# One layer of a mixed-sequence encoder on one core: the S5 outputs and their gate placed beside the recurrent chain, the gate's result kept on chip, the two halves of the mixing exchanged

## Chip, cores and metric

One core of a Trainium2 chip. The metric is the device time of one execution in microseconds (us), median of several runs. The kernel as it stood takes 880.22 us (three runs, 878.32 to 882.06).

## What is computed

One encoder layer in float32 over 512 tokens of width 1024, with a memory of 256 tokens. Cut to what matters here:

```
h = rmsnorm(x) ; u, q, k, v, z, beta, a = split(h @ w_in)
# S5: two linear recurrences (forward, backward) over u, then
y = scan_f(u) + scan_b(u) + d * u
g = gelu(y)
y_s5 = rmsnorm(g * sigmoid(g @ w_glu + b_glu))              # 512 x 512
# gated delta net: 4 heads of 128, chunks of 64, both directions
for each chunk:  v_new = u_i - w_i @ S
                 o_i   = (q_i * exp(g_i)) @ S + qk_i @ v_new
                 S     = S * exp(g_last) + k_i' @ v_new
y_gdn = rmsnorm_per_head(o_f + flip(o_b)) * silu(z)         # 512 x 512
x = x + concat(y_s5, y_gdn) @ w_out                         # "the mixing"
x = x + cross_attention(rmsnorm(x), rmsnorm(mem))
x = x + hierarchical_moe(rmsnorm(x))                        # 32 experts, 2 per token
out = rmsnorm(x)
```

## The kernel before

The program is written as generators that each yield after a small piece of work. `weave((g1, n1), (g2, n2), ...)` (L44) draws from them in the ratio of the numbers, and this gives the program order. The order on each engine is then set by a scheduler in the kernel's build, which takes program order as priority and moves an instruction ahead where its own model finds an engine free; it also places the tiles, in pools on four stacks (`left`, `r1`, `r2`, `r3`; a pool opened where another was closed reuses its place, and its first write waits for the last readers of what lay there). Each engine then runs its list in order, and so does SP's list, which holds nearly all the DMA issues.

The part of the program around the change, in program order:

1. **The chain** (`gdn_chain`, L818 on): 8 chunk steps of the delta net, each in two half-steps of two heads. In each, PE forms k^T S and q^T S (L863), DVE the right-hand side `r` (L864), PE multiplies with the inverted chunk matrix `lhc` (L869), ACT copies to `vn` (L870), PE forms the state update (L880), DVE adds it (L883). It uses PSUM banks 3 to 7. `out(b)` (L824 to L838) forms the block's output with 16 small matmuls of `qkd` and `vn` (L831, L832) and calls `gdn_out` (L897 to L917): square (ACT, L904), reduce (DVE, L905, L906), a power on POOL (L907), a product (DVE, L908), four transposes (PE, L911), the load of the gate `zs` from scratch (one buffer `ozs`, L915), the product (DVE, L916) and the store of the result to `gd_scr[b]` (L917). Blocks 1 and 2 come out after the seventh step, 0 and 3 after the eighth.
2. Beside it in the weave: the memory's keys and values (`mem_kv`: weights of `xa_wk` and `xa_wv` through the ring `wst`, PE L163) and the S5 recurrence (`s5_rec`, 62 steps on DVE, L441 to L444). Ratio 20 to 9 to 47.
3. After the weave `r1` is closed. **`s5_out`** (L447 on): 8 groups `gg`, each with one load `cal` (L453), ACT and POOL work that lays out `hc` (L463, L464) and 12 matmuls (L473 to L475) with the tables `tz`; these come in two halves of eight loads each (L457, one buffer), and then 16 transposes (L484) give `gt`. It uses PSUM banks 0 and 1.
4. **`mix_weights`** for the delta-net half of `w_out`: 8 pieces, each a load `mst` (SP, L930), a high part (ACT, L931) and a low part (POOL, L932).
5. **`s5_glu`** (L491 on): 4 rounds `m` of 4 matmuls with `wglu` (L502), a sigmoid (ACT, L504), a product (DVE, L506), a square (ACT, L508), 4 matmuls with ones (L510), a scaled copy (ACT, L512) and a store to `s5_scr[m]` (L513).
6. **The mixing**: `mix_act` loads each block back (L944) and splits it in a high part (ACT, L945) and a low part (DVE, L946); `mix` makes 12 matmuls of 512 columns per block and half of the output (L169 to L171). First the delta-net half, 4 blocks by 2 halves; then the `r` stacks are closed, the S5 half's activations and weights are loaded and split (4 `mxs`, 8 `mst`), and the S5 half is mixed, together with the transposes for the cross-attention (`xattn_in`).

Of the kernel before, what the change touches and what calls it, by code (L numbers as in the profile page):

```python
# [9 lines left out]
F32 = mybir.dt.float32  # L10
# [54 lines left out]
class Enc:  # L65
# [85 lines left out]
    def wsplit(self, src, w, lo_eng):  # L151

        st = self.wcols(src, w)
        hi = self.wp.tile([P, 8, w], F32R, name="whi", bufs=2)
        lo = self.wp.tile([P, 8, w], F32R, name="wlo", bufs=2)
# [18 lines left out]
    def stage_a(self):  # L174
# [5 lines left out]
        with tc.tile_pool(name="xp", bufs=1) as xp:  # L180
# [8 lines left out]
            def first_weights():  # L189
                for c0 in (0, P):  # L190
                    self.pre[c0] = self.wsplit(self.w_in(c0, P), P, nc.gpsimd)
                self.w_g = self.wp.tile([P, 8, 16], F32, name="wg", bufs=1)
# [14 lines left out]
    def proj_u(self):  # L207
        nc = self.nc
        scr = self.u_scr
        for m in range(4):  # L210
            ps = self.proj(m * P)
            u = self.wp.tile([P, 8, 64], F32, name="ut", tag="ut", bufs=1)
# [278 lines left out]
    def s5_glu(self):  # L491
        nc, sp, A = self.nc, self.s5g, self.A
        gt = self.gt
        wg = sp.tile([P, 4, T], F32, name="wglu")
# [4 lines left out]
        for m in range(4):  # L499
# [3 lines left out]
            sg = sp.tile([P, T], F32, name="sg")  # L503
            nc.scalar.activation(sg, ps, AF.Sigmoid, bias=bglu[:, m:m + 1])  # L504
            s5 = sp.tile([P, T], F32, name="s5g")
            nc.vector.tensor_tensor(s5, gt[:, m, :], sg, op=OP.mult)  # L506
            sq = sp.tile([P, T], F32, name="s5q")
# [4 lines left out]
            nc.scalar.activation(s5, s5, AF.Copy, scale=n5[:, m:m + 1])  # L512
            nc.sync.dma_start(self.s5_scr[m], s5)  # L513
# [191 lines left out]
    def proj_z(self):  # L705
        nc = self.nc
        for h in range(4):
            ps = self.proj(2048 + h * P, nc.gpsimd)
            z = self.wp.tile([P, T], F32, name="zt", tag="ut", bufs=1)
# [264 lines left out]
    def mem_kv(self):  # L974
# [3 lines left out]
        for which, w in ((0, wk), (1, wv)):  # L978
            for n in range(8):
                ps = self.ps("mm")  # L980
                self.mm8(ps[:, :256], self.wcols(w[:, :, n * P:(n + 1) * P], P), self.mt)
                o = self.wp.tile([P, 256], F32, name="kvo", bufs=2)
                nc.scalar.activation(o, ps[:, :256], AF.Copy)
                if which:
# [3 lines left out]
                    o = self.wp.tile([P, 256], F32, name="kvt", bufs=2)  # L988
# [547 lines left out]
    def build(self):  # L1536
# [6 lines left out]
        self.s5_scr = [scr(f"s5_scr{i}", (P, T)) for i in range(4)]  # L1543
# [58 lines left out]
        weave((self.gdn_chain(), 20), (kv, 9), (rec, 47))  # L1602
        r1.close()
# [3 lines left out]
        self.set_banks(s5=(0, 1))  # L1607
        for _ in self.s5_out():
            pass
        r3.close()  # L1610
        wgd = self.mix_weights(pool(r3, "mw", **rt), 512, 2)
        left.close()
        for _ in self.s5_glu():
            pass
# [8 lines left out]
        with tc.tile_pool(name="ma", bufs=1) as ma, tc.tile_pool(name="mo", bufs=1) as mo:  # L1623
            blk = (1, 2, 0, 3)
            act = self.mix_act(ma, [((slice(0, 4), slice(b * P, (b + 1) * P)), self.gd_scr[b]) for b in blk])
            for b in blk:
                for n in range(2):
                    self.mix(xs, act, wgd, b, n, None)
            for r in (r3, r2, r0):
                r.close()  # L1630
# [176 lines left out]
```

## Time and profile before

| what | value |
|---|---|
| median of three runs | 880.22 us (878.32 to 882.06) |
| the profiled execution | 872.87 us, of which the span from its first to its last instruction is 871.1 us |
| PE busy in the span | 771.9 us, 89% |
| DVE, ACT, POOL busy | 422.1, 348.3 and 180.3 us |
| mean granted TensorE clock | 0.932 of full speed |
| bytes moved | 185.21 MB, 213 GB/s on average |

The profiled execution lies 0.8% below the median. Times in the trace count from the start of its span, so a sum made on the trace stands against 872.87 us, and the same difference is then put on the median. PE is the busiest engine, but the busy share is an average over stages: up to about 594 us the matmuls set the pace, behind that the stream of expert weights. "Granted clock" is the share of full clock pulses that TensorE was given; it moves between two levels, 1.2 and 2.4 GHz, so 0.5 to 1.00 in the rows. One float32 matmul of the program stands as two records of PE. A line number of the changed kernel is larger by 3 in the chain's code (L869 becomes L872), by 5 in the gate's first lines and 3 behind.

### The profile page before, as it was taken

Reading aid. Unit: us, or ns where it says so; the run is one execution under the profiler, and the core shown is the slowest. Engines: PE = TensorE matmul, PEld = TensorE weight load, DVE = VectorE, ACT = ScalarE, POOL = GpSimd, SP = SyncE. Lnnn points to the kernel's source line nnn. Section 1 sums busy time; section 2 is a strip of 40 time slices with the busy share of each in tenths; the row PEclk is TensorE's granted clock in tenths of the full one; section 3 lists DMA queues with packets and bytes.
Section 4 is the critical chain, followed back from the end, with each engine's and each line's share of the span. In section 5 each row is a group of like instructions: output and inputs, shape, how many; then the busy total and the mean of one; then the engine's idle time right before and its main releaser. Section 6 shows DMA issues by size and latency. Waiting matters only on the chain. (4 is left out here: it accounts for less than half of the span.)

```text
span 871.1 us, 13365 instructions
## 1 busy us (share of the span) xinstructions
PE 771.9 (89%) x4911; PEld 533.1 (61%) x4912; DVE 422.1 (48%) x1100; ACT 348.3 (40%) x783; POOL 180.3 (21%) x189
## 2 busy tenths in 40 slices
PE   4989889989989998998999999992998788887983
PEld 3668777768888676775788789992433333332431
DVE  5389999989979422425452644216000000000375
ACT  6465666644143454533334544432322312112204
POOL 3010312342011121132151332323111111101203
PEclk9989999999969977967999999996899999998997
DMA  7929233245623375135646314983999999999982
GB/s 210 154 74 198 85 96 103 77 163 196 193 85 97 62 174 99 44 120 162 184 158 218 121 49 169 335 326 138 324 410 416 413 410 407 404 390 411 412 316 99
DMA packets 128133, 185.21 MB, mean 213 GB/s; under 512 B 38734, under 2 KB 93006, under 8 KB 123968
## 3 DMA queue, kind: packets, MB, share of 16 engines
q1 hardware_dynamic: 122736, 172.31, 59.1%
q0 software_dynamic: 5328, 12.01, 3.7%
q8 instruction: 40, 0.66, 0.3%
q14 instruction: 29, 0.24, 0.1%
HBM read 165.50 MB, written 26.18 MB: 220 GB/s over the span
## 5 line engine op out<-in xcount | busy, mean ns | idle before, releaser
L1369 PE MATMUL bank<-mw,xt 128*64 128x512 f32 x360 | 106.4, 604 | 1.9 <-DMA mw<-in_moe_w_up_dram 1.9
L1373 DVE SCALAR_TENSOR_TENSOR hs<-hs,tw,bank 128x256 f32<-128x256 f32 x16 | 7.7, 481 | 170.5 <-ACT hs L1372 170.5
L1372 ACT ACTIVATE hs<-bank,tw 128x256 f32<-128x256 f32 x16 | 7.6, 473 | 157.8 <-PE bank L1369 157.8
L169 PE MATMUL bank<-htl,whi 128*128 128x512 f32 x160 | 66.1, 414 | 4.4 <-ACT cv L666 2.0
L1369 PEld LDWEIGHTS bank<-mw,xt 128*64 128x64 f32 x360 | 33.3, 140 | 58.2 <-issue 57.0
L171 PE MATMUL bank<-hth,wlo 128*128 128x512 f32 x160 | 64.1, 402 | 0.0
L170 PE MATMUL bank<-hth,whi 128*128 128x512 f32 x160 | 64.0, 400 | 0.0
L1409 PE MATMUL bank<-mw,hT 128*64 128x512 f32 x152 | 48.8, 646 | 16.2 <-ACT yd L1414 16.2
L163 PE MATMUL bank<-mt,wst 128*128 128x256 f32 x256 | 58.9, 387 | 0.0
L1001 POOL TENSOR_TENSOR wlo<-wst,whi 128x1024 fp32r<-128x1024 f32 x16 | 38.6, 2417 | 78.7 <-ACT whi L1000 78.7
L163 PEld LDWEIGHTS bank<-mt,wst 128*128 128x128 f32 x256 | 49.0, 195 | 6.9
L1349 POOL DMA_INDIRECT xg<-t_scr,tidx x16 | 16.5, 1029 | 137.4 <-PE bank L1356 134.4
L668 DVE SCALAR_TENSOR_TENSOR cv<-xp,taps,cv 128x512 f32<-128x512 f32 x48 | 39.3, 829 | 0.1
L169 PEld LDWEIGHTS bank<-htl,whi 128*128 128x128 f32 x160 | 31.0, 194 | 13.4 <-ACT cv L666 2.9
L883 DVE SCALAR_TENSOR_TENSOR S<-S,egl,bank 128x128 f32<-128x128 f32 x48 | 15.8, 346 | 46.8 <-PE bank L880 46.8
L1359 ACT ACTIVATE xt<-bank,gm 128x128 f32<-128x128 f32 x128 | 34.7, 382 | 9.0 <-PE bank L1356 7.9
L169 PE MATMUL bank<-wlo,oh 128*128 128x256 f32 x128 | 36.6, 289 | 0.0
L1409 PEld LDWEIGHTS bank<-mw,hT 128*64 128x64 f32 x152 | 13.6, 146 | 37.6 <-issue 19.6
L853 POOL TENSOR_TENSOR kt<-kn,kd 64x512 f32<-64x512 f32 x14 | 14.5, 1036 | 105.0 <-PE bank L880 57.8
L170 PE MATMUL bank<-whi,oh 128*128 128x256 f32 x128 | 35.8, 283 | 0.0
L171 PE MATMUL bank<-whi,ol 128*128 128x256 f32 x128 | 35.3, 287 | 0.0
L171 PEld LDWEIGHTS bank<-hth,wlo 128*128 128x128 f32 x160 | 30.7, 192 | 6.6
(545 smaller groups left out, 1969.4 us busy)
## 6 DMA issues: line engine op xcount, KB each, us to landing
mw<-in_moe_w_down_dram SPq DMA_DIRECT2D x23, 1024.0 KB, 13.2
mw<-in_moe_w_gate_dram SPq DMA_DIRECT2D x45, 512.0 KB, 13.8
mw<-in_moe_w_up_dram SPq DMA_DIRECT2D x45, 512.0 KB, 13.9
wst<-in_w_in_dram SPq DMA_DIRECT2D x20, 512.0 KB, 5.0
ca_scr<-ca SPq DMA_DIRECT2D x8, 512.0 KB, 2.7
wst<-in_xa_wk_dram SPq DMA_DIRECT2D x8, 512.0 KB, 4.3
y_scr<-lhc SPq DMA_DIRECT2D x2, 2048.0 KB, 10.6
wst<-in_xa_wv_dram SPq DMA_DIRECT2D x8, 512.0 KB, 4.2
```

Of the source, the lines that this page charges most:

```text
L163: self.nc.tensor.matmul(ps, w[:, k, :], act[:, k, :], start=(k == 0), stop=(k == 7))
L169: self.nc.tensor.matmul(ps, ah, bl, start=(first and i == 0), stop=False)
L170: self.nc.tensor.matmul(ps, ah, bh, start=False, stop=False)
L171: self.nc.tensor.matmul(ps, al, bh, start=False, stop=(last and i == n - 1))
L668: v.scalar_tensor_tensor(cv, xp[:, w:w + T], taps[:, w, m:m + 1], cv, op0=OP.mult, op1=OP.add)
L853: nc.gpsimd.tensor_tensor(kt[s], self.kn[s, ch // 2], self.kd[s, ch // 2, di * 4:di * 4 + 4, None].to_broadcast([64, 4, P]), op=OP.mult)
L883: v.scalar_tensor_tensor(sn, S[di, h], self.egl[:, ch % 2, ch // 2, di * 4 + h:di * 4 + h + 1], p, op0=OP.mult, op1=OP.add)
L1001: nc.gpsimd.tensor_tensor(lo, st, hi.bitcast(F32), op=OP.subtract)
L1349: self.gather = g_.indirect_dma_start(out=xg, out_offset=None, in_=self.t_scr, in_offset=bass.IndirectOffsetOnAxis(ap=self.tidx[:, q:q + 1 ...
L1359: nc.scalar.activation(xt[:, k], ps[:, (k % 4) * P:(k % 4 + 1) * P], AF.Copy, scale=self.gm[:, k:k + 1])
L1369: nc.tensor.matmul(pg[w * 64:w * 64 + 64].rearrange("p (a n) -> p a n", a=2), xt[:, k, w * 64:w * 64 + 64], un[k // 4 * 2 + w][:, :, k % 4 ...
L1409: nc.tensor.matmul(py[w * 64:w * 64 + 64], hT[:, k, w * 64:w * 64 + 64], wd[w][:, k, c], start=(k == 0), stop=(k == 1))
```

## The change

The S5 pools are opened before the chain's weave, and a third stream `s5_side` is woven beside the chain: the rest of the recurrence, `s5_out`, the rest of `mem_kv`, `s5_glu`. For that S5 gets one PSUM bank (2, which the chain's `out` uses too) in place of two, and some tiles move from the pool `wp` to `pa`, so that the stack `r2` is free before the chain. The gate's result is no longer stored and loaded back: its high and low part are formed on chip, in the place of the recurrence's `U`, and `wglu` and the temporaries take the places of `uperm` and `mt`. The S5 half of `w_out` is now the first to be loaded, into `r3` behind the weave, the delta-net half comes second, and the mixing begins with the S5 half.

```diff
@@ s5_glu
-        wg = sp.tile([P, 4, T], F32, name="wglu")
+        act = self.s5p.tile([P, 2, 4, T], F32R, name="s5a", tag="U")
+        hi, lo = self.act5 = act[:, 0], act[:, 1]
+        wg = self.s5p.tile([P, 4, T], F32, name="wglu", tag="uperm")
+        tmp = self.mp.tile([P, 4, T], F32, name="glt", tag="mt")
+        sg, sq = tmp[:, 0], tmp[:, 1]
...
-            sg = sp.tile([P, T], F32, name="sg")
             nc.scalar.activation(sg, ps, AF.Sigmoid, bias=bglu[:, m:m + 1])
-            s5 = sp.tile([P, T], F32, name="s5g")
+            s5 = tmp[:, 2 + m % 2]
...
-            nc.scalar.activation(s5, s5, AF.Copy, scale=n5[:, m:m + 1])
-            nc.sync.dma_start(self.s5_scr[m], s5)
+            nc.scalar.activation(hi[:, m], s5, AF.Copy, scale=n5[:, m:m + 1])
+            nc.vector.scalar_tensor_tensor(lo[:, m], s5, n5[:, m:m + 1], hi[:, m].bitcast(F32), op0=OP.mult, op1=OP.subtract)
@@ the main program
         self.set_banks(ch=(3, 4, 5, 6, 7), out=(2,), tp=(1,), mm=(0,))
-        weave((self.gdn_chain(), 20), (kv, 9), (rec, 47))
-        r1.close()
         self.s5g = pool(r2, "s5g", **rt)
         self.s5o = pool(r3, "s5o", **rt)
-        self.set_banks(s5=(0, 1))
-        for _ in self.s5_out():
-            pass
+        self.set_banks(s5=(2,))
+        def s5_side():
+            for i, _ in enumerate(rec):
+                if i % 8 == 7:
+                    yield
+            yield from self.s5_out()
+            for _ in kv:
+                yield
+            yield from self.s5_glu()
+        weave((self.gdn_chain(), 20), (kv, 14), (s5_side(), 26))
         r3.close()
-        wgd = self.mix_weights(pool(r3, "mw", **rt), 512, 2)
+        w5 = self.mix_weights(pool(r3, "mw", **rt), 0, 2)
         left.close()
-        for _ in self.s5_glu():
-            pass
...
+            for n in range(2):
+                for b in range(4):
+                    self.mix(xs, self.act5, w5, b, n, self.s5r)
             act = self.mix_act(ma, [((slice(0, 4), slice(b * P, (b + 1) * P)), self.gd_scr[b]) for b in blk])
-            for b in blk:
-                for n in range(2):
-                    self.mix(xs, act, wgd, b, n, None)
-            for r in (r3, r2, r0):
+            wgd = self.mix_weights(mo, 512, 4)
+            for r in (r3, r2, r1, r0):
                 r.close()
...
-            act = self.mix_act(mo, [((k, slice(0, T)), self.s5_scr[k]) for k in range(4)])
-            w5 = self.mix_weights(mo, 0, 4)
             for n in range(2):
-                for b in range(4):
-                    self.mix(xs, act, w5, b, n, self.s5r)
-                    if n and b == 0:
+                for b in blk:
+                    self.mix(xs, act, wgd, b, n, None)
+                    if n and b == blk[0]:
                         self.xattn_in(xs, 0)
```

How the built program's lists stand at three places. First **PE at the chain's end**, from the last products with `lhc` to the first matmul of the mixing (`gt,wglu` is the gate, `ones,...` its sums of squares, `vn,qkd` the chain's outputs, `ident,ot` their transposes). Before:

```order
L502 MATMUL bank_4064<-gt,wglu 128x512 x4
L869 MATMUL bank_2802<-r,lhc 128x128
L832 MATMUL bank_3643<-vn,qkd 64x128
L831 MATMUL bank_3643<-vn,qkd 64x128
L510 MATMUL bank_4046<-ones,s5q 128x1 x4
L911 MATMUL bank_3551<-ident,ot 128x128 x4
L832 MATMUL bank_3643<-vn,qkd 64x128
L510 MATMUL bank_4064<-ones,s5q 128x1 x4
L831 MATMUL bank_3706<-vn,qkd 64x128
...
L911 MATMUL bank_3672<-ident,ot 128x128 x4
L911 MATMUL bank_3724<-ident,ot 128x128 x4
L169 MATMUL bank_4124<-mlo,mxh 128x512
```

and now:

```order
L872 MATMUL bank_2836<-r,lhc 128x128 x2
L835 MATMUL bank_3950<-vn,qkd 64x128
L834 MATMUL bank_3950<-vn,qkd 64x128
L914 MATMUL bank_3786<-ident,ot 128x128 x4
...
L507 MATMUL bank_3796<-gt,wglu 128x512 x4
L513 MATMUL bank_3796<-ones,glt 128x1 x4
L507 MATMUL bank_3840<-gt,wglu 128x512 x4
L513 MATMUL bank_3840<-ones,glt 128x1 x4
...
L914 MATMUL bank_3886<-ident,ot 128x128 x4
L914 MATMUL bank_3979<-ident,ot 128x128 x4
L507 MATMUL bank_3896<-gt,wglu 128x512 x4
L914 MATMUL bank_4019<-ident,ot 128x128 x4
```

Behind the last product with `lhc` there stand now three of the gate's four rounds (none before), 35 products `vn,qkd` (11 before; the second "..." stands for 24 of them) and four sets of transposes (three before); the four sums, the third round's and the mixing follow.

Second, **SP's list from the chain's end on** (`mst` the pieces of `w_out`, `ozs` the gate of a block, `gd_scr` and `mxs` its store and the load back). Before:

```order
L930 DMA mst<-in_w_out_dram 128x512 x4
L513 DMA s_scr<-s5g 128x512
L930 DMA mst<-in_w_out_dram 128x512 x2
L917 DMA gd_scr<-oy 128x512
L915 DMA ozs<-z_scr 128x4x128
L930 DMA mst<-in_w_out_dram 128x512
L513 DMA s_scr<-s5g 128x512
L930 DMA mst<-in_w_out_dram 128x512
```

and now:

```order
L947 DMA mxs<-gd_scr 128x512
L920 DMA gd_scr<-oy 128x512
L918 DMA ozs<-z_scr 128x4x128
L947 DMA mxs<-gd_scr 128x512
L920 DMA gd_scr<-oy 128x512
L933 DMA mst<-in_w_out_dram 128x512 x2
L947 DMA mxs<-gd_scr 128x512
L933 DMA mst<-in_w_out_dram 128x512 x14
```

Before, the first eight pieces stand around the first block's store (and the other eight behind the fourth block's); now all 16 stand behind the store of the fourth and last block.

Third, **POOL's list**, the low parts of the weights (`mlo`). Before:

```order
L907 TENSOR_TENSOR ors<-oss,nhalf 128x4
L932 TENSOR_TENSOR mlo<-mst,mhi 128x512 x8
L907 TENSOR_TENSOR ors<-oss,nhalf 128x4
L1174 IOTA io_4486 128x64
...
L907 TENSOR_TENSOR ors<-oss,nhalf 128x4
L932 TENSOR_TENSOR mlo<-mst,mhi 128x512 x8
L1001 TENSOR_TENSOR wlo<-wst,whi 128x1024 x2
```

and now, with numbers (`mlo_4035` and `mlo_4053` the S5 half, columns 0 to 511 and 512 to 1023; `mlo_4225` and `mlo_4243` the delta-net half):

```order
L935 TENSOR_TENSOR mlo_4035<-mst_4036,mhi_4034 128x512
L935 TENSOR_TENSOR mlo_4035<-mst_4040,mhi_4034 128x512
L935 TENSOR_TENSOR mlo_4225<-mst_4226,mhi_4224 128x512
...
L935 TENSOR_TENSOR mlo_4035<-mst_4048,mhi_4034 128x512
L935 TENSOR_TENSOR mlo_4243<-mst_4244,mhi_4242 128x512
...
L935 TENSOR_TENSOR mlo_4053<-mst_4066,mhi_4052 128x512
L1004 TENSOR_TENSOR wlo_4540<-wst_4537,whi_4539 128x1024
```

Before, eight stand between the first and the second block's power and eight behind the fourth's; now all 16 stand behind the fourth's, the S5 half's last four at the end.

## Rows read from the trace of the kernel before

**Rows 1.** Busy time by stage: stretch, length, then each engine, granted clock, DMA share, GB/s
```profile
300.00:345.00 45.00, 38.09 (x307) 29.07 (x308) 11.47 (x37) 23.65 (x43) 7.21 (x16) 0.77 0.74 151
365.20:400.70 35.50, 35.50 (x155) 23.18 (x154) 11.70 (x22) 15.00 (x28) 11.10 (x9) 0.81 0.28 89
400.70:414.66 13.96, 9.91 (x54) 8.06 (x52) 8.27 (x19) 4.18 (x7) 4.11 (x9) 0.63 0.82 255
414.66:462.40 47.74, 47.74 (x210) 38.99 (x210) 21.35 (x29) 14.04 (x21) 15.71 (x10) 0.96 0.49 156
500.00:594.50 94.50, 92.81 (x647) 83.66 (x645) 30.86 (x71) 38.37 (x90) 25.70 (x13) 1.00 0.63 229
```

**Rows 2.** The page's GB/s in 40 equal slices of the span
```profile
GB/s 210 154 74 198 85 96 103 77 163 196 193 85 97 62 174 99 44 120 162 184 158 218 121 49 169 335 326 138 324 410 416 413 410 407 404 390 411 412 316 99
```

**Rows 3.** Chain products with `lhc` on PE: ns min/median/max, first and last start
```profile
L869 PE MATMUL bank<-r,lhc x56: 272/377/582, 278.5 to 400.8; 128*128 128x128 f32 x56
...
L869 PE MATMUL bank<-vc,lhc x8: 272/274/275, 263.0 to 276.6; 128*128 128x128 f32 x8
```

**Rows 4.** PE's waits from 263 to 414.7: us in total, times, longest
```profile
PE bank L911 <- DVE ot L908: 3.7, 2, 2.9
...
PE bank L473 <- issue: 1.7, 1, 1.7
...
PE bank L473 <- DMA tz<-w_scr: 1.1, 1, 1.1
```

**Rows 5.** Last DVE step of the recurrence; first `s5_out` products; loads of `tz`
```profile
L444 DVE TENSOR_TENSOR U<-U,rt x57: 213/224/1076, 203.1 to 287.4; 128x64 f32<-128x64 f32 x57
...
L473 PE MATMUL bank<-tz,uperm x64: 272/273/476, 311.2 to 355.5; 128*64 128x128 f32 x64
L457 SPq DMA_DIRECT2D tz<-w_scr x16: 318/447/518, 298.9 to 327.8; - x16
```

**Rows 6.** PE in order of time from 395 to 415: start, us, what
```profile
395.44 5.42 PE L502 MATMUL bank<-gt,wglu 128*128 128x512 f32 x12
...
405.97 0.63 PE L831 MATMUL bank<-vn,qkd 64*64 64x128 f32 x2
...
408.11 0.63 PE L832 MATMUL bank<-vn,qkd 64*64 64x128 f32 x2
...
413.58 1.12 PE L911 MATMUL bank<-ident,ot 128*128 128x128 f32 x4 [0.84 <-DVE ot L908]
414.66 0.76 PE L169 MATMUL bank<-mlo,mxh 128*128 128x512 f32 x1
```

**Rows 7.** Groups from 400.7 to 462.4: count, busy us, mean ns, idle before
```profile
L916 DVE SCALAR_TENSOR_TENSOR oy<-bank,gng,ozs 128x512 f32<-128x512 f32 x3 | 2.3, 751 | 0.1
...
L506 DVE TENSOR_TENSOR s5g<-gt,sg 128x512 f32<-128x512 f32 x1 | 0.7, 711 | 0.2 <-DMA s_scr<-s5g 0.2
...
L504 ACT ACTIVATE sg<-bank,c_s_b_glu 128x512 f32<-128x512 f32 x1 | 0.7, 687 | 0.6 <-PE bank L502 0.6
```

**Rows 8.** SP's list in order of time, from 355 to 445
```profile
364.16 6.52 SPq L930 DMA_DIRECT2D mst<-in_w_out_dram  x4
...
416.16 0.53 SPq L915 DMA_DIRECT2D ozs<-z_scr  x1
...
422.67 0.32 SPq L917 DMA_DIRECT2D gd_scr<-oy  x1
424.84 0.32 SPq L944 DMA_DIRECT2D mxs<-gd_scr  x1
...
433.28 4.54 SPq L930 DMA_DIRECT2D mst<-in_w_out_dram  x4
```

**Rows 9.** All loads of `ozs`: us from issue to landing
```profile
DMA to landing us min/median/max: 3.1/4.6/8.1
```

**Rows 10.** All loads of `mst`: us from issue to landing
```profile
DMA to landing us min/median/max: 2.5/2.9/5.6
```

**Rows 11.** POOL in order of time: the second eight low parts of `w_out`
```profile
431.95 10.95 POOL L932 TENSOR_TENSOR mlo<-mst,mhi 128x512 fp32r<-128x512 f32 x8 [19.16 <-DMA mst<-in_w_out_dram]
```

More of the change, by code (lines that the diff above doesn't have):

```diff
@@ L153, in wsplit @@
         st = self.wcols(src, w)
-        hi = self.wp.tile([P, 8, w], F32R, name="whi", bufs=2)
-        lo = self.wp.tile([P, 8, w], F32R, name="wlo", bufs=2)
+        hi = self.pa.tile([P, 8, w], F32R, name="whi", bufs=2)
+        lo = self.pa.tile([P, 8, w], F32R, name="wlo", bufs=2)
         self.nc.scalar.activation(hi, st, AF.Copy)
@@ L191, in first_weights @@
                     self.pre[c0] = self.wsplit(self.w_in(c0, P), P, nc.gpsimd)
-                self.w_g = self.wp.tile([P, 8, 16], F32, name="wg", bufs=1)
+                self.w_g = self.pa.tile([P, 8, 16], F32, name="wg", bufs=1)
                 nc.sync.dma_start(self.w_g, self.w_in(2560, 16))
@@ L211, in proj_u @@
             ps = self.proj(m * P)
-            u = self.wp.tile([P, 8, 64], F32, name="ut", tag="ut", bufs=1)
+            u = self.pa.tile([P, 8, 64], F32, name="ut", tag="ut", bufs=1)
             nc.scalar.activation(u.rearrange("p j k -> p k j"), ps.rearrange("p (k j) -> p k j", j=8), AF.Copy)
@@ L502, in s5_glu @@
                 nc.tensor.matmul(ps, wg[:, k, m * P:(m + 1) * P], gt[:, k, :], start=(k == 0), stop=(k == 3))
-            sg = sp.tile([P, T], F32, name="sg")
             nc.scalar.activation(sg, ps, AF.Sigmoid, bias=bglu[:, m:m + 1])
-            s5 = sp.tile([P, T], F32, name="s5g")
+            s5 = tmp[:, 2 + m % 2]
             nc.vector.tensor_tensor(s5, gt[:, m, :], sg, op=OP.mult)
-            sq = sp.tile([P, T], F32, name="s5q")
             nc.scalar.activation(sq, s5, AF.Square)
@@ L708, in proj_z @@
             ps = self.proj(2048 + h * P, nc.gpsimd)
-            z = self.wp.tile([P, T], F32, name="zt", tag="ut", bufs=1)
+            z = self.pa.tile([P, T], F32, name="zt", tag="ut", bufs=1)
             nc.scalar.activation(z, ps, AF.Silu)
@@ L981, in mem_kv @@
                 self.mm8(ps[:, :256], self.wcols(w[:, :, n * P:(n + 1) * P], P), self.mt)
-                o = self.wp.tile([P, 256], F32, name="kvo", bufs=2)
+                o = self.wp.tile([P, 256], F32, name="kvo", tag="kvo", bufs=2)
                 nc.scalar.activation(o, ps[:, :256], AF.Copy)
@@ L987, in mem_kv @@
                         nc.tensor.transpose(pt[:, m * P:(m + 1) * P], o[:, m * P:(m + 1) * P], self.ident)
-                    o = self.wp.tile([P, 256], F32, name="kvt", bufs=2)
+                    o = self.wp.tile([P, 256], F32, name="kvt", tag="kvo", bufs=2)
                     nc.scalar.activation(o, pt[:, :256], AF.Copy)
@@ L1542, in build @@
         self.z_scr = scr("z_scr", (P, 4, T))
-        self.s5_scr = [scr(f"s5_scr{i}", (P, T)) for i in range(4)]
         self.gd_scr = [scr(f"gd_scr{i}", (P, 4, P)) for i in range(4)]
```

## Prediction

> **What bounds the kernel now.** I first read the busy time by stage. From 263 us to the end of the mixing PE has work almost all the time: 38.09 of 45.00 us from 300, all of the 35.50 us from 365.2, 9.91 of 13.96 us from 400.7, all of the 47.74 us of the mixing [rows 1]. So that stretch is set by PE, by its order and its clock: the granted clock is 0.77, 0.81 and 0.63 in the three stretches ahead of the mixing. Behind it there is no slack to absorb a shift: PE is busy 92.81 of 94.50 us in the cross-attention [rows 1], then expert weights stream at about 410 GB/s to the end [rows 2], from places that come free only step by step. So whatever the change does to the mixing's end I pass on to the kernel's end one for one.
>
> Two times frame the edit. The chain's last product with `lhc` is L = 400.8, the first is at 263.0 [rows 3]. The mixing ends at 462.4, 61.6 us after L, of which 13.9 us lie ahead of its first matmul at 414.66 [rows 6] and 47.7 us are the mixing itself [rows 1].
>
> PE's waits say what is not PE work [rows 4]: 3.7 us for the last head outputs, 1.7 and 1.1 us at `s5_out` for its tables. The list of `s5_out` tells what a place beside the chain could bring: the recurrence ends at 287.4, but the first product comes at 311.2, because the table loads were only issued from 298.9 on [rows 5]. SP's list and POOL's low parts tell what the tail costs: the first eight pieces of `w_out` are issued from 364.16, long before they are needed; the other eight come at the end, up to 433.28 [rows 8], and POOL is through with them 10.95 us after 431.95, while PE still mixes the delta-net half [rows 11].
>
> **The change part by part.**
>
> *S5 outputs earlier.* The table loads are no longer behind the last keys-and-values store, so `s5_out` can start when the recurrence is done, near 291 in place of 311. That is a gain for L only where PE had nothing to do. From 263.0 to L are 137.8 us. Of these some 7 us were idle (the waits of rows 4 and their small companions, less the 3.7 behind L), and the low clock took 45.00 x 0.23 + 35.50 x 0.19 = 17 us [rows 1]. So about 114 us are work at full clock.
>
> *Work that goes behind L.* In the changed list three of the gate's four rounds and 24 more of the 64 output products stand behind the last `lhc`. A round is 8 records at 5.42/12 us, 3.6 us [rows 6]. An output product took (408.11 - 405.97)/5 = 0.43 us at the lower clock level [rows 6], 0.22 at the higher. That is 10.8 + 5.3 + about 1 for sums and transposes: 17 us. So 97 us remain ahead of L, and L would be 360 with no stall at all, and 384 if all 24 us of idle and low clock came back. The second half of `tz` still waits for the first to be read (one buffer), and the one PSUM bank of S5 lets one group at a time through. I take 377, two thirds of that loss: L is 24 us earlier.
>
> *The tail from L to the last store, T.* Here the rows of before don't show the new arrangement, so I build it from pieces. The 11 products and four transposes that stand first: 3.4 us. Two gate rounds follow, each on the same bank: 3.6 us of matmuls, then sigmoid, product and square of about 0.7 each [rows 7], the sums and a copy that frees the bank, about 4 us with the hand-offs; together 15.2. Then 24 products, 5.3 us, of blocks that could have gone out before. From the last product to the last transposes it took 414.7 - 408.7 = 6.0 us [rows 6]; with one more block about 7. That makes 31. The three blocks then go through one `ozs` buffer in turn: product 0.75 [rows 7], store and load issue, landing 4.6 us [rows 9], product, the same again, then the last store, which was through 424.84 - 422.67 = 2.2 us after its issue [rows 8]: 0.75 + 2 x (0.9 + 4.6 + 0.75) + 2.2 = 15.5. T - L is 47 us at full clock. If all PE pieces ran at the lower level, 15.5 us of them would double: 62. The stretch of before that is most like it, 13.96 us with PE 71% busy, had 0.63 [rows 1]; I take 54. Before, the last store's reader started at 424.84; now T = 377 + 54 = 431.
>
> *The weights.* This is what makes the tail expensive. The pool of the first-needed weights takes over a place that the chain's own tiles hold, and in SP's list all 16 `mst` loads stand behind the fourth block's store. SP runs in order, so the first load starts at T. Before, eight were hidden beside the chain [rows 8]. First low part: T + 2.9 for landing [rows 10] + 0.6 on ACT + 10.95/8 = 1.37 on POOL [rows 11] = T + 4.9. Sixteen low parts take 21.9 us on POOL; with two buffers for the S5 half three of them also wait for a new load, about 3 us together, so the last is ready at T + 28.4. POOL's order puts the S5 half's last four at the end, so PE can't finish the S5 half before T + 28.4 + 47.74/16 = T + 31.4. The delta-net half behind it costs 47.74/2 = 23.9 us [rows 1], its transposes included. The mixing ends at T + 55.3. Bounds: T + 52.6 if POOL never waits and PE sets the pace (4.9 + 47.74), T + 62 if PE's gaps hold the clock down in the first half.
>
> *Stores and loads removed.* Four stores, four loads, four ACT and four DVE passes go. They cost nothing: their reads ran while PE was mixing the delta-net half without a gap (47.74 of 47.74 [rows 1]). The four added DVE passes of 0.75 us cost nothing, as DVE has room there. The Trainium skill ("DMA: Bandwidth & Descriptors", the anatomy of one DMA) gives each DMA a fixed cost of about 2 us, most of it the write receipt; eight on the path would be an estimated 16 us saved and the forecast would fall to about 888.
>
> *Sum.* New end of the mixing: 377 + 54 + 55.3 = 486.3 against 462.4: **24 us later**. On the profiled execution that is 872.9 + 24 = 897; that execution was 7 us under the median, so the median becomes 880.2 + 24 = 904.
>
> **The rivals.**
>
> A. *PE stays fed and the early start pays in full (faster or same).* With S5 work always at hand beside the chain, PE has no gaps, the clock stays at the upper level and L falls to 360. For it: 24 us were lost there [rows 1, 4]. The tail at full clock, 47, and the mixing at PE's pace, 52.6, end at 459.6, 3 us earlier than before: 877; the last 2 to 3 us for "faster" would have to come from a tail whose head outputs overlap more than I assume (874). It decides if L lies below about 362. Against it: in 365 to 400 PE had no idle time at all and still got 0.81 [rows 1]. The Trainium skill ("TensorE: Matmul & The Clock Gate", on loop structure) ties the rate to how continuously PE is fed, which is this rival's ground; the row with full busy time at 0.81 doesn't bear it out alone.
>
> B. *Only the weights are exposed (smaller loss).* Head outputs overlap the gate and ozs lands in 3.1 us [rows 9]: T - L = 41. Then 377 + 41 + 54 = 472, 10 us later: 890. Against it: PE's list puts the 24 products behind the second gate round.
>
> C. *The clock stays low (larger loss).* The tail's matmuls come in short bursts between ACT passes. L 381, T - L 62, mixing 62: 505, 43 us later: 923. For it: 0.63 ahead of the mixing [rows 1].
>
> D. *The change doesn't do what it says.* The scheduler had already put `s5_out` and the gate beside the chain [rows 3, 5, 6], so L might hardly move while the tail grows: 392 + 50 + 55.3 = 497, 35 us later: 915.
>
> **How the numbers follow.** Forecast 0.58 (about 895 to 912), A 0.10, B 0.14, C 0.09, D 0.09. The range 885 to 921 leaves out A, and the upper part of C. A measurement of this kernel tells 0.5% (4.4 us) from no change: of A's 0.10 half is faster than 875.8 and half within; the edge of B adds 0.01 to "same". The rest is slower.
>
> **What would show it.** Right: L near 377, the first `s5_out` product near 291; behind L three gate rounds with PE waiting on ACT between them; the first `mst` load after the last `gd_scr` store, near 431; 16 low parts on POOL one behind the other; PE waiting for `mlo` in the first half of the mixing; the mixing's end near 486 and the last part unchanged in length. Wrong: an `mst` load before L; L below 362 with a granted clock of 1.00; a tail under 40 us; or a stage behind the mixing that gives the shift back.

## The result, and the profile after

The changed kernel takes 884.56 us (median of 20 runs, 879.60 to 899.00), the kernel before, on the same chips, 879.99 us (20 runs, 871.24 to 893.27). Some runs were one to two per cent longer at a lower granted clock, and the ratio leaves them out: it is **1.0054, with a 95% interval of 1.0028 to 1.008**, half a per cent slower, some 5 us. Forecast were 904 us, with a range of 885 to 921. The sign held; the size was about five times too large, and the time lies just below the range.

The profiled execution of the changed kernel took 881.89 us, its span 880.1 us. Against the span of before, 871.1 us, that is 9.0 us more. The trace of before, which the sum was made on, lies 7 us under its kernel's median, the trace of after 3 us; so of the 9.0 us between the two traces only about half is a difference of the kernels.

Busy time by stage of the kernel after (stretch, length, engines, granted clock, DMA share, GB/s):

```profile
300.00:345.00 45.00, 40.63 (x361) 31.19 (x357) 12.93 (x41) 24.62 (x54) 8.55 (x18) 0.89 0.43 109
345.00:371.10 26.10, 25.64 (x186) 18.64 (x186) 12.69 (x32) 10.44 (x26) 1.03 (x1) 1.00 0.00 1
371.10:416.40 45.30, 32.14 (x131) 20.86 (x130) 20.10 (x35) 9.68 (x17) 4.19 (x9) 0.77 0.37 108
416.40:448.60 32.20, 27.10 (x104) 21.24 (x105) 7.16 (x13) 10.98 (x18) 21.13 (x17) 0.84 0.42 139
448.60:472.00 23.40, 23.40 (x113) 19.59 (x112) 8.17 (x13) 4.55 (x6) 4.75 (x2) 1.00 0.34 113
510.00:604.00 94.00, 93.17 (x649) 84.00 (x647) 30.93 (x70) 38.57 (x92) 25.54 (x12) 1.00 0.63 229
```

The stretches end at the chain's last product with `lhc` (371.1), at the first load of `w_out` (416.4), at the end of the S5 half and at the end of the mixing (472.0). The chain's end came 29.7 us earlier than in [rows 3]; the mixing's end (471.9) came 9.5 us later than in [rows 1]. Between them lies a stretch of 45.3 us in which PE is busy for 32.14 at a clock of 0.77, and then 32.2 us of which POOL is busy for 21.13. Cross-attention is as long as before (94.00 us against 94.50 [rows 1]).

The chain's products with `lhc` (ns min/median/max, first and last start), which answer to [rows 3]:

```profile
L872 PE MATMUL bank<-r,lhc x56: 272/275/582, 280.5 to 371.1; 128*128 128x128 f32 x56
```

PE from the chain's end to the mixing, in order of time (start, us, what; in brackets the idle time ahead of it and what ended it), which answers to [rows 6]:

```profile
374.34 3.70 PE L507 MATMUL bank<-gt,wglu 128*128 128x512 f32 x8
380.26 1.05 PE L513 MATMUL bank<-ones,glt 128*128 128x1 f32 x8 [2.23 <-ACT glt L511]
381.73 5.40 PE L507 MATMUL bank<-gt,wglu 128*128 128x512 f32 x8 [0.42 <-DVE gss L514]
389.50 1.05 PE L513 MATMUL bank<-ones,glt 128*128 128x1 f32 x8 [2.37 <-ACT glt L511]
...
400.54 0.63 PE L835 MATMUL bank<-vn,qkd 64*64 64x128 f32 x2
403.25 1.08 PE L914 MATMUL bank<-ident,ot 128*128 128x128 f32 x4 [2.09 <-DVE oss L909]
405.12 1.12 PE L914 MATMUL bank<-ident,ot 128*128 128x128 f32 x4 [0.78 <-DVE ot L911]
406.03 5.34 PE L507 MATMUL bank<-gt,wglu 128*128 128x512 f32 x8
412.58 0.66 PE L914 MATMUL bank<-ident,ot 128*128 128x128 f32 x4 [1.21 <-DVE ot L911]
416.10 1.70 PE L513 MATMUL bank<-ones,glt 128*128 128x1 f32 x8 [2.87 <-ACT glt L511]
421.26 0.79 PE L169 MATMUL bank<-mlo,s5a 128*128 128x512 f32 x1 [3.45 <-POOL mlo L935]
```

Two rounds of the gate with ACT between them, then the blocks' products up to 400.5, then the transposes: three blocks' outputs stand behind the gate. Each round waits over 2 us for its square (L511). At 421.26 it is POOL's low part that PE waits for.

SP's list in the same stretch, which answers to [rows 8]:

```profile
405.88 0.33 SPq L920 DMA_DIRECT2D gd_scr<-oy  x1
...
410.13 0.32 SPq L920 DMA_DIRECT2D gd_scr<-oy  x1
...
414.32 0.32 SPq L920 DMA_DIRECT2D gd_scr<-oy  x1
416.43 0.81 SPq L933 DMA_DIRECT2D mst<-in_w_out_dram  x2
417.33 0.38 SPq L947 DMA_DIRECT2D mxs<-gd_scr  x1
417.75 20.86 SPq L933 DMA_DIRECT2D mst<-in_w_out_dram  x14
```

No piece of `w_out` is loaded before 416.43; before the change eight of them were under way from 364.16. POOL's low parts, which answer to [rows 11]:

```profile
419.94 2.51 POOL L935 TENSOR_TENSOR mlo<-mst,mhi 128x512 fp32r<-128x512 f32 x2 [0.43 <-DMA mst<-in_w_out_dram]
423.25 15.01 POOL L935 TENSOR_TENSOR mlo<-mst,mhi 128x512 fp32r<-128x512 f32 x12 [0.80 <-DMA mst<-in_w_out_dram]
```

14 of the 16 follow each other almost without a gap, and the last ends at 443. PE's waits for them (us in total, times, longest):

```profile
PE bank L169 <- POOL mlo L935: 5.1, 2, 3.4
```

The longer one is the wait ahead of the first product, at 421.26; behind it PE waits for POOL only once more, for 1.6 us.

### The profile page after: what moved, and what is told of

The parts are those of the page before. It is cut to its first block, busy times and chain, and to the rows that moved or that the text cites. A ratio compares the mean times of both kernels' runs of the same rounds, so it can differ in the third digit from the quotient of the medians.

```text
span 880.1 us, 13327 instructions
## 1 busy us (share of the span) xinstructions
PE 765.2 (87%) x4911; PEld 529.8 (60%) x4912; DVE 419.9 (48%) x1100; ACT 346.6 (39%) x779; POOL 181.0 (21%) x189
## 5 line engine op out<-in xcount | busy, mean ns | idle before, releaser
L1412 PE MATMUL bank<-mw,hT 128*64 128x512 f32 x152 | 50.6, 660 | 16.3 <-ACT yd L1417 16.3
L163 PEld LDWEIGHTS bank<-mt,wst 128*128 128x128 f32 x256 | 48.5, 193 | 11.4 <-issue 5.1
L671 DVE SCALAR_TENSOR_TENSOR cv<-xp,taps,cv 128x512 f32<-128x512 f32 x48 | 37.2, 784 | 0.3 <-ACT cv L669 0.2
L170 PEld LDWEIGHTS bank<-hth,whi 128*128 128x128 f32 x160 | 30.8, 193 | 5.8
```

The source lines that it names most:

```text
L163: self.nc.tensor.matmul(ps, w[:, k, :], act[:, k, :], start=(k == 0), stop=(k == 7))
L170: self.nc.tensor.matmul(ps, ah, bh, start=False, stop=False)
L671: v.scalar_tensor_tensor(cv, xp[:, w:w + T], taps[:, w, m:m + 1], cv, op0=OP.mult, op1=OP.add)
L1412: nc.tensor.matmul(py[w * 64:w * 64 + 64], hT[:, k, w * 64:w * 64 + 64], wd[w][:, k, c], start=(k == 0), stop=(k == 1))
```

## The experiments

Two theories stood at the start. **W**: the loss is the weights, which can only be loaded behind the last block's store. **G**: the loss is the gate, whose rounds wait for each other on one bank behind the chain and hold the blocks' outputs back. All twelve in one table, on their profiled executions; "ratio" is that of the timed runs to the kernel before.

| kernel | last `lhc` | last block's store | first `w_out` load | last mixing product | span | ratio (95%) |
|---|---|---|---|---|---|---|
| before | 400.8 | 422.7 | 364.2 | 462.1 | 871.1 | 1 |
| the change | 371.1 | 414.3 | 416.4 | 471.7 | 880.1 | 1.0054 (1.0028 to 1.008) |
| e1 weights early | 370.9 | 417.9 | 345.7 | 457.7 | 869.1 | 0.9906 (0.9864 to 0.9948) |
| e2 gate behind outputs | 360.5 | 388.7 | 390.8 | 462.9 | 872.9 | 1.0008 (0.9969 to 1.0047) |
| e3 low parts on two | 366.3 | 412.2 | 414.3 | 467.4 | 874.4 | 1.018 (1.007 to 1.029) |
| e4 early, gate ahead | 385.1 | 432.9 | 336.8 | 465.5 | 873.2 | 1.0001 (0.9962 to 1.004) |
| e5 gate on two banks | 388.0 | 407.1 | 409.2 | 464.4 | 874.3 | 0.9955 (0.9918 to 0.9993) |
| e6, e9 early, gate outside | 382.0 | 410.1 | 347.0 | 443.3 | 850.0 | 0.9788 (0.9734 to 0.9843) |
| e7 halves back | 371.4 | 416.6 | 418.8 | 477.3 | 887.7 | 1.0158 (1.0109 to 1.0206) |
| e8 through DRAM | 368.2 | 414.1 | 416.2 | 473.8 | 883.1 | 1.0119 (1.0066 to 1.0172) |
| e10 gate outside, late | 385.9 | 407.6 | 409.8 | 465.3 | 875.6 | 0.9969 (0.994 to 0.9999) |
| e11 before, late | | | | | | 1.0193 (1.0156 to 1.0231) |
| e12 early, through DRAM | 382.3 | 402.3 | 346.0 | 456.0 | 865.4 | 0.9932 (0.9896 to 0.9969) |

(The row of e6 and e9 shows e9's trace. Of e11's trace only the order of SP's list is used, no time. The mixing products are given by their starts.) From the last mixing product to the end it is 406.7 to 411.4 us in all traces of the table, while that product moves over 34 us: what the mixing's end does is passed on.

### e1: the weights' place alone

Where the tiles lie shows where the wait came from: the changed kernel's pool of the first weights begins at byte 135,936 of a partition, and the chain's tiles reach up to 143,616, an overlap of 7,680 bytes. In e1 the pool has 28 KB in place of 36, beginning at 144,128, and the low parts of the second half-width go to the ring `wst`, which is idle by then.

```diff
-        w5 = self.mix_weights(pool(r3, "mw", **rt), 0, 2)
+        w5 = self.mix_weights5(pool(r3, "mw", **rt))
...
+            hi = pool.tile([P, 4, 512], F32R, name="mhi", bufs=2)
+            if n == 0:
+                t = pool.tile([P, 4, 512], F32R, name="mlo", bufs=1)
+                lo = [t[:, k] for k in range(4)]
+            else:
+                t = [self.wp.tile([P, 2, 512], F32R, name="mlw", tag="wst", bufs=3) for _ in range(2)]
+                lo = [t[k // 2][:, k % 2] for k in range(4)]
```

> Only the place of the S5 half's weights is changed: it no longer overlaps the chain's tiles, so all eight pieces can be loaded and split as soon as the S5 outputs are done. The order of PE's other work stays. Theory W (the loss is the weights that start only behind the last block's store): the eight loads stand before the last product with lhc, PE no longer waits for their low parts, some 27 of the 96 S5 products fill gaps of the gate, and the mixing ends near 458, 14 us before the changed kernel's 471.9: some 867 to 872, ratio to before near 0.99. Theory G (the loss is the gate's three rounds and the outputs behind the chain): the S5 products only fill, the head outputs still end 45 us behind the chain, and no more than 5 us come back: 877 to 880, ratio 0.997 to 1.00.

870.15 us (10 runs), ratio 0.9906; the last mixing product at 457.7, 14.0 us earlier, as W had it. SP's list of e1:

```profile
345.72 17.52 SPq L954 DMA_DIRECT2D mst<-in_w_out_dram  x8
...
417.88 0.32 SPq L920 DMA_DIRECT2D gd_scr<-oy  x1
420.09 0.32 SPq L968 DMA_DIRECT2D mxs<-gd_scr  x1
420.51 1.98 SPq L933 DMA_DIRECT2D mst<-in_w_out_dram  x4
```

The S5 half's eight pieces are loaded from 345.72, and only the other eight stand behind the last store, which is 3.6 us later than in the changed kernel. So the gate and the outputs were as slow as in the changed kernel, and 14 us came back all the same: without the wait of W the change is no loss. That the gate has no part in the loss does not follow; e2, e5 and e10 come back to it.

### e11: the same wait put into the kernel before

```diff
-        wgd = self.mix_weights(pool(r3, "mw", **rt), 512, 2)
+        mw = pool(r3, "mw", **rt)
+        pad = mw.tile([P, 2048], F32, name="pad")
+        nc.vector.memset(pad[:, 0:4], 0.0)
+        wgd = self.mix_weights(mw, 512, 2)
```

> The kernel before with one edit: its first weights' pool is made 8 KB longer by an unused tile, so that it reaches into the chain's tiles, as in the changed kernel. Nothing else of the change is in it. Theory W: the first eight loads leave 364 and go behind the last store near 424, and the mixing ends 13 to 18 us later than 462.4: 888 to 896, ratio 1.012 to 1.02. If the weights' start doesn't count: 1.00 within 0.4%.

895.35 us (5 runs), ratio 1.0193 (1.0156 to 1.0231), in the upper part of what W gave. An unused tile of 8 KB costs the kernel before 1.9%. The weights' own tiles lie where they lay before, from byte 144,192; only the pool reaches lower, to 136,000, and in SP's list all 16 loads stand behind the last store. So the wait goes by the pool, not by the tile. With e1 this shows the cause from both sides: the wait alone makes a kernel slower, by 1.9% here, and without it the change is no loss.

### e7 and e8: the two other parts of the change undone

e7 puts the halves back in their old order; with that, the first transposes for the cross-attention come behind both halves in program order, where they stood inside the second:

```diff
-        w5 = self.mix_weights(pool(r3, "mw", **rt), 0, 2)
+        wgd = self.mix_weights(pool(r3, "mw", **rt), 512, 2)
...
+            for b in blk:
+                for n in range(2):
+                    self.mix(xs, act, wgd, b, n, None)
+            w5 = self.mix_weights(mo, 0, 4)
             for n in range(2):
                 for b in range(4):
                     self.mix(xs, self.act5, w5, b, n, self.s5r)
...
             for n in range(2):
-                for b in blk:
-                    self.mix(xs, act, wgd, b, n, None)
-                    if n and b == blk[0]:
-                        self.xattn_in(xs, 0)
+                if n:
+                    self.xattn_in(xs, 0)
```

> The changed kernel with only the halves of the mixing exchanged back: the delta-net half's weights first and mixed first, the S5 half behind it. Theory W: these weights take the same place and wait for the same last store, so the time stays that of the changed kernel within 4 us, 879 to 887. A rival, that the exchange of the halves itself costs the time (the delta-net half's loads were hidden before, so putting it first should hide them again): back to the kernel before, 874 to 879, with mst loads ahead of the chain's end.

889.02 us (6 runs), ratio 1.0158. The rival fell: the first load stood at 418.8, behind the last store again. But the time is not the changed kernel's either. From the first load to the last mixing product it is 58.5 us in place of 55.3, and the first load itself was 2.3 us later. Behind the last mixing product it needs 2.0 us more (410.4 against 408.4), where PE now waits 1.95 us behind the late transposes. So the exchange of the halves is a gain of its own, about 3 us on the traces and up to 1% by the ratios; how much of that is the transposes' place was not tried.

e8 stores the gate's result and loads it back:

```diff
-            nc.scalar.activation(hi[:, m], s5, AF.Copy, scale=n5[:, m:m + 1])
-            nc.vector.scalar_tensor_tensor(lo[:, m], s5, n5[:, m:m + 1], hi[:, m].bitcast(F32), op0=OP.mult, op1=OP.subtract)
+            nc.scalar.activation(s5, s5, AF.Copy, scale=n5[:, m:m + 1])
+            nc.sync.dma_start(self.s5_scr[m], s5)
...
+            self.act5 = self.mix_act(mo, [((k, slice(0, T)), self.s5_scr[k]) for k in range(4)])
```

> The changed kernel with the gate's result stored and loaded back as in the kernel before (four stores, four loads, four ACT and four DVE passes more, four fused DVE passes less). Theory W: hidden behind the weights, so within 2 us of the changed kernel, 880 to 885. By the fixed cost of a DMA that the Trainium skill states, if one store and load stood on the path, about 4 us more: 886 to 890.

889.48 us (6 runs), ratio 1.0119 (1.0066 to 1.0172), whose interval meets that of the change (1.0028 to 1.008). The last mixing product is 2.1 us later. The round trip was nearly hidden on the trace; whether it costs 2 us or the 5 to 6 of the ratios stays open.

### e2, e5, e10: the gate and the outputs, weights as changed

e2 takes the gate out of the weave, so that it follows the chain in program order; e5 leaves it there and gives it banks 0 and 1; e10 does both.

```diff
-            yield from self.s5_glu()
...
+        for _ in self.s5_glu():
+            pass
         r3.close()
```

```diff
+            self.set_banks(s5=(0, 1))
             yield from self.s5_glu()
```

(The first diff is e2's, the second e5's; e10 has the first with the banks set ahead of its loop.)

> The changed kernel with the gate out of the weave, in program order behind the chain, so that the head outputs go first and all four rounds of the gate follow; the weights' place stays as changed. Theory G in its form 'the outputs wait behind the gate': the last store moves from 45 us behind the chain's last product to about 28, the weights start as much earlier, and the mixing ends 12 to 18 us before 471.9: 866 to 872. Theory W: the weights still start behind the last store and cost the same 31 us to the end of the S5 half, so the gain is that of the store alone, also 12 to 18 us. If instead the rounds themselves are what counts (one more of them is now behind the chain), no gain or a loss of up to 8 us: 882 to 890.

876.17 us (10 runs), ratio 1.0008. The store came 28.2 us behind the chain's end, as G had it, and the loads 25.6 us earlier than in the changed kernel, but the mixing's end only 8.8, short of the 12 to 18 expected. The loads no longer set it then: the last of the gate's results came at 421.5, and the S5 half ended at 439.3, 48.5 us behind the first load.

> The changed kernel with the gate alone on two PSUM banks (0 and 1, which keys and values no longer use by then) in place of one; weights as changed. Theory G (the gate's rounds wait for each other on one bank and hold the outputs back): the rounds move ahead of the chain's last product, which comes some 8 to 11 us later, and the last store follows it after 26 to 30 us in place of 45, near 408; the weights start there, and the mixing ends near 464, 8 us before 471.9: 872 to 877. If PE's work and its clock alone set the tail: the last store stays within 3 us of 416 and the time within 3 us of the changed kernel's 882.

873.17 us (10 runs), ratio 0.9955, last mixing product at 464.4, where 464 was expected. The rounds moved ahead of the chain's end (at 388.0), and the last store followed 19 us behind it. Behind it the bill of W is the same: 409.2 to 464.4 is 55.2 us. Busy time by stage of e5:

```profile
345.00:388.00 43.00, 43.00 (x277) 28.80 (x276) 21.07 (x50) 17.74 (x38) 2.04 (x2) 1.00 0.04 13
388.00:409.20 21.20, 6.52 (x52) 5.11 (x51) 12.92 (x23) 3.40 (x6) 4.14 (x9) 0.73 0.69 206
409.20:464.60 55.40, 48.45 (x208) 39.11 (x209) 13.84 (x20) 15.27 (x23) 24.84 (x18) 0.92 0.40 129
```

PE is full and at full clock up to the chain's end, and then has nothing to do for 14.7 of 21.2 us: for 8.3 of them it waits for the outputs' passes on DVE, the rest is the start of its wait for the weights. The S5 products, which could fill both, have no weights yet.

> The same without the earlier weights (their place as in the changed kernel; gate behind the chain in program order, on two banks). Theory W: the last store near 407, all 16 loads behind it, the mixing's end 55 us later, near 462: 868 to 876, some 15 to 20 us more than with the weights early. If the gate's and outputs' order alone made the ninth run fast: within 5 us of it.

873.97 us (10 runs), ratio 0.9969; last mixing product at 465.3, 55.5 us behind the first load. As W had it, though 3 us later than the 462 expected. With banks of its own the gate runs ahead of the chain's end here as well, whatever its place in program order: its last product with `wglu` starts at 376.3, the chain's last with `lhc` at 385.9.

So the loss has two handles. In e5 and e10 the weights still wait for the last store, but the store comes 7 us earlier (407.1 and 407.6 against 414.3), the mixing's end 7 and 6 us earlier, and neither is slower than the kernel before (0.9955 and 0.9969). W says what the mixing's end hangs on, the last store; how late that comes is the gate's and the outputs' doing, as G has it.

### e6, e9 and e12: the parts together

e6 is e1 with e10's gate:

```diff
-        w5 = self.mix_weights(pool(r3, "mw", **rt), 0, 2)
+        w5 = self.mix_weights5(pool(r3, "mw", **rt))
...
-            yield from self.s5_glu()
...
+        self.set_banks(s5=(0, 1))
+        for _ in self.s5_glu():
+            pass
```

> The first experiment's place for the weights, the gate in program order behind the chain, and the gate on two banks. Theories W and G together: S5 weights ready before the chain's end, outputs not behind the gate, the last store near 408, S5 products in the gaps, and the delta-net weights' low parts ready some 14 us behind the last store; the mixing ends near 442, 16 us before the first experiment's 458: 850 to 860. If, as in the fourth run (mixing's end at 465.8 where 445 to 450 was expected), S5 products get ahead of the head outputs and the delta-net weights then start late, it ends at 455 to 466: 867 to 876.

857.7 us (4 runs, 850.77 to 865.06; kernel before 876.1), without an interval; e9 repeats it.

> The sixth experiment's kernel once more, with more rounds, for an interval: its mixing ended at 441.1, 30.8 us before the changed kernel's and 21.3 before that of the kernel before. If the stretch behind the mixing is passed on one for one, 852 to 862, ratio to before 0.970 to 0.985.

The edit is e6's. 859.53 us (6 runs), ratio **0.9788 (0.9734 to 0.9843)**: faster than the kernel before by about 2% (1.6 to 2.7), and by its ratio faster than the changed kernel as well. Its runs spread widely, from 851.81 to 870.19; why was not tried. Busy time by stage of e9, to its last store's reader and to the mixing's end:

```profile
345.00:382.00 37.00, 36.53 (x250) 25.91 (x249) 20.61 (x42) 18.40 (x39) 11.53 (x9) 1.00 0.23 72
382.00:412.70 30.70, 30.70 (x155) 23.69 (x155) 19.65 (x37) 5.77 (x10) 5.18 (x10) 1.00 0.47 143
412.70:443.50 30.80, 27.62 (x122) 22.42 (x121) 9.05 (x14) 10.11 (x15) 14.81 (x10) 0.94 0.51 163
```

In the stretch that had 32.14 of 45.30 us at 0.77 in the changed kernel, PE is busy for 30.70 of 30.70 at 1.00: S5 products fill the time in which the blocks' outputs go through ACT, POOL, DVE and the one `ozs` buffer. The low parts of the delta-net half, still behind the last store, cost one wait of 3.2 us. e10 differs from e9 by the weights' place alone: 22.0 us at the mixing's end, 1.8% by the ratios.

e12 is e9 with e8's edit (the store to `s5_scr` and `mix_act` in place of the result kept on chip):

```diff
-            nc.scalar.activation(hi[:, m], s5, AF.Copy, scale=n5[:, m:m + 1])
-            nc.vector.scalar_tensor_tensor(lo[:, m], s5, n5[:, m:m + 1], hi[:, m].bitcast(F32), op0=OP.mult, op1=OP.subtract)
+            nc.scalar.activation(s5, s5, AF.Copy, scale=n5[:, m:m + 1])
+            nc.sync.dma_start(self.s5_scr[m], s5)
```

> The ninth run's kernel with the gate's result through DRAM again. There the weights no longer hide the round trip, and S5 products can't fill the gate's gaps, since the loads back stand behind the last store in SP's list: the mixing starts near 411 and ends near 457, 16 us later than 441: 868 to 876. If the round trip is hidden there too, as in the eighth run: within 4 us of the ninth run.

868.28 us (10 runs), ratio 0.9932; last mixing product at 456.0, where 457 was expected. PE's waits in e12 from 263 to 480 (us in total, times, longest):

```profile
PE bank L912 <- DVE ot L909: 8.5, 3, 8.0
PE bank L169 <- ACT mxh L967: 6.5, 1, 6.5
```

PE waits for the outputs and for what was loaded back, 15.0 us, which S5 products filled in e9. So the result kept on chip, worth 2 us on the trace of the changed kernel, is worth 12.7 with the weights out of the way (1.4% by the ratios).

### e4 and e3: two misses

e4 is e1 with another weight in the weave, which brings the whole gate to the chain's end or ahead of it:

```diff
-        weave((self.gdn_chain(), 20), (kv, 14), (s5_side(), 26))
+        weave((self.gdn_chain(), 20), (kv, 14), (s5_side(), 52))
```

> The first experiment's weights and a weave weight of 52 in place of 26 for the S5 stream, so that all four rounds of the gate and part of the S5 half's products stand before the chain's last product. Both theories together: that last product comes 8 to 14 us later than 371, the last store about 30 us behind it, and the mixing ends near 445 to 450: 855 to 862, ratio near 0.98. If PE's own work sets the end (the low clock, theory C), what is moved ahead of the chain's end is only paid there: 870 to 880.

876.65 us (10 runs), ratio 1.0001: 15 to 22 us more than expected. The last store came 47.8 us behind the chain's end in place of 30. PE's waits in e4 from 345 to 466:

```profile
PE bank L914 <- DVE ot L911: 5.8, 2, 5.0
PE bank L169 <- POOL mlo L935: 4.7, 1, 4.7
```

S5 products now stood in PE's list ahead of the blocks' outputs (54 of them lie between the chain's end and the last block's transposes); so the last store went to 432.9, the delta-net half's weights, which wait for it, to 435.3, and W's bill came with the other half. The time lies in the range that the expectation gave to a limit by PE's own work, but PE's work alone was not the limit: from 385.00 to 435.30 it was busy for 40.68 of 50.30 us, at a clock of 0.76.

e3 lets DVE make every second low part:

```diff
-                nc.gpsimd.tensor_tensor(lo[:, k], st, hi[:, k].bitcast(F32), op=OP.subtract)
+                (nc.vector if k % 2 else nc.gpsimd).tensor_tensor(lo[:, k], st, hi[:, k].bitcast(F32), op=OP.subtract)
```

> The changed kernel with every second low part of the weights on DVE in place of POOL. Theory W with POOL as its pace: the S5 half of the mixing runs at PE's pace from its first product, and its end comes 4 to 6 us earlier: 877 to 879. If the loads or PE's clock set that pace: no change within 1 us.

In time it is inconclusive: 888.21 us in 4 runs (876.26 to 898.03), and the profiled one was the fastest of them. On its trace the mixing's last product comes 4.3 us earlier, but half of that is an earlier last store; from the first load to the last mixing product 2.2 us were gained, 53.1 in place of 55.3.

## Why the prediction was right in kind and wrong in size

**The mechanism held.** The weights stood behind the last store, so the mixing's end hung on T, the time of the first load, and the rest shifted along. T + 55.3 was the forecast for the mixing's end; it came at T + 55.5 (471.9 against 416.4). The last mixing product starts 55.3 us behind the first load in the changed kernel, 55.2 in e5 and 55.5 in e10. That the sum came so close is in part luck. POOL was through at T + 26.7, not T + 28.4; the S5 half ended 5.5 us behind that, not 3.0; the delta-net half took 23.3, not 23.9. POOL did not pace the S5 half to its end either: behind the first product PE waited for it once, for 1.6 us, and from 421.26 to 425.20 its granted clock was 0.50, by an estimate from these two numbers another 2 us. e11 shows that the wait alone makes a loss, e1 that without it the change is no loss; e5 and e10 show that an earlier last store takes the loss back too.

What failed is the size of three terms: the loss ahead of the chain's end L, the tail from L to T, and the base that the sum was put on.

**The chain's end, "I take 377, two thirds of that loss": 371.1.** Work left ahead of it was sized right (97 us): of the 106.0 us from the first product at 265.1 PE was idle for 6.1 and lost 5 to the clock (45.00 x 0.11), which leaves 95. What was wrong is the loss: 11 us, not 17. The second half of `tz` did cost a wait, 3.6 us, but from 345 to the chain's end the clock was 1.00, where before it had been 0.81 from 365.2 on, and from 300 to 345 it was 0.89 in place of 0.77. Off by 6 us.

**The tail, "I take 54": 45.3, below the 47 given as its lower end.** Up to the last product `vn,qkd` it was right (400.5 is 29.4 us behind the chain's end; 24 at full clock and some of the 7 added). Then the sum had the first of the three stores wait for all transposes, 7.75 us behind that product's end (401.2); it came 4.7 us behind it, at 405.88, with the last transposes still to come at 412.58. And the three stores stood 4.2 us apart (405.88, 410.13, 414.32), not 6.25: the two loads of `ozs` between them landed in 3.0 and 2.9 us. All four loads of the kernel after:

```profile
DMA to landing us min/median/max: 2.9/3.1/7.3
```

The sum took the median of before, 4.6 [rows 9]. Of the eight loads in the two traces the slowest, 8.1 and 7.3 us, were in flight while 314 and 329 GB/s moved, the two of this tail while some 180 did; another of before took 5.6 at 164, so traffic is not all of it. The minimum of the row, 3.1, was the right price for this tail. Off by 9 us: 4 by the stores' spacing, 3 of these by the landing, and 3 by the overlap of stores and transposes.

**The base, "so the median becomes 880.2 + 24".** With these two terms right the sum on the trace would have been 371.1 + 45.3 + 55.3 - 462.4 = 9.3 us; the spans differ by 9.0. The timed runs show about 5. The sum was put on the median as if the changed kernel's profiled execution would also lie 7 us under its median; it lay within 3 us of it (881.89 against 884.56). So some 4 us of the traces' 9 are an execution well under the median on one side. That is argued from the spread; no second trace of before was taken.

**The rivals.** A (PE stays fed, L at 360) had its clock from 345 to the chain's end, but neither its chain's end (371.1, where it needed less than 362) nor its time: L fell by 30 us and the mixing still ended later. PE stayed fed in e9, with L at 382.0, where it was busy all the time behind the chain as well. There the rule of the Trainium skill ("TensorE: Matmul & The Clock Gate", "Loop structure matters more than you think": keep matmuls back to back while loads run beside them) agrees with the rows: 1.00 from 345.00 to 412.70 against 0.77 in the changed kernel's tail. B came nearest in time (890): of its two conditions one held, the landing of `ozs` in 3.1 us, and so its T - L of 41 was close to 45.3; the outputs did not overlap the gate but stood behind it. C did not happen (T - L was 45.3, not 62), nor D: L moved by 30 us, and the first `hc` products started at 292.9, not 311.6.

**What was costed at nothing.** The round trip through DRAM was hidden as long as the weights were late (2.1 us on the trace), and is worth 12.7 us where they are not. The exchange of the halves was not priced at all, and gives some 3 us by e7.

So the gain of the earlier chain's end went into a new wait: by the ratios the weights' place costs about 13 us (1.0054 against 0.9906), and without it the change is 0.9% faster than the kernel before.

## What to carry to other kernels

When a pool is opened behind a stage, look at the bytes it takes, not only at the line it stands in: here 7.5 KB of overlap with the tiles of the stage's last step turned loads that had been hidden into the end of the path, and an unused tile that overlaps them by as much does the same to a kernel that is otherwise unchanged. Ask also what that end waits for: by the ratios, taking the wait away gave 1.5% (e1), bringing the last store forward 1.0% (e5), and both together 2.7% (e9). What a transfer or an on-chip result is worth depends on what else is late; undo it once with and once without the other waits. And take a price for a load from rows with the traffic that it will meet, and a sum from an execution whose time is near the median.

## What was not expected of the hardware

DVE's low parts were slowed beside POOL's in e3. A subtraction of 128x512 took DVE 693 ns in the kernel before (the median of its `mxl` passes), and 1201 in e3, where POOL makes its own at the same time. The low parts of e3 (ns min/median/max):

```profile
L935 POOL TENSOR_TENSOR mlo<-mst,mhi x8: 1263/1303/1744, 417.9 to 435.0; 128x512 fp32r<-128x512 f32 x8
L935 DVE TENSOR_TENSOR mlo<-mst,mhi x8: 959/1201/1595, 418.6 to 435.8; 128x512 fp32r<-128x512 f32 x8
```

POOL's median rose little, 1295 to 1303, DVE's by 73%. The kernel before shows the same without any edit: six of its eight `mxl` passes took 0.69 us each, and the last two, which run from 434.57 inside POOL's stretch of [rows 11], 3.44 us together. The Trainium skill ("SBUF — State Buffer", "SBUF: two separate sides") says that the two share a pair of ports which one holds for a whole instruction; a DVE pass that waits for part of one of POOL's fits these rows. So half of the low parts on DVE was not half of the time.
